# Attention scores as 64-row products of two heads in turn, with the softmax in pairs of heads

## The chip, the cores and the metric

The kernel runs on one core of a Trainium2 chip. The metric is the device time of one execution in microseconds (us); a time given for a kernel is the median of its runs. The engines have short names: PE is TensorE, DVE is VectorE, ACT is ScalarE, POOL is GpSimd, and SP (SyncE) issues the DMA transfers.

## The reference

One layer of a mixer with 128 context tokens and 512 latent tokens (8 grid rows of 64), model width 1024. A modulated RMS norm feeds one input projection; three branches read it: attention of 8 heads x 64, a gated linear recurrence, and a Fourier mixing. Each branch is gated, and one output projection, a norm and a residual follow. The change concerns the attention's scores:

```python
def one_row(r):                       # a row of the latent grid
    q_r = lax.dynamic_index_in_dim(qg, r, axis=1, keepdims=False)
    k_r = lax.dynamic_slice_in_dim(kg, r0, kh, axis=1)
    ...
    s_lat = jnp.einsum('bqhd,bjkhd->bhqjk', q_r, k_r).astype(jnp.float32) * scale
    s_lat = s_lat + bias.transpose(0, 2, 1, 3)[None].astype(jnp.float32)
    s_lat = jnp.where(col_in[:, None, :], s_lat, -jnp.inf)
    s_ctx = jnp.einsum('bqhd,bphd->bhqp', q_r, k_ctx).astype(jnp.float32) * scale
    s = jnp.concatenate([s_lat.reshape(B, H, GRID_W, kh * GRID_W), s_ctx], axis=-1)
    p = jax.nn.softmax(s, axis=-1).astype(v.dtype)
```

Everything is in float32. The 128 context tokens attend to themselves in the same way without a bias.

## The kernel before, in words

All 640 tokens are worked on together. Numbers that TensorE multiplies are kept as two parts, a main part `hi` in a rounded format and the rest `lo`; a product is then three products, hi x hi, hi x lo and lo x hi, added up in PSUM. `split` makes the two parts, a cast for the main part and a subtraction for the rest.

The program is written as streams (Python generators) that an object `Order` merges by an estimate of time: the start (modulation and norm), the recurrence, the attentions of four pairs of heads (`attention(p)`, p = 0 to 3), the gate vectors, and `fill`, which brings in the blocks of the input projection in the order of the string `FILL` and then the output projection. A block of the projection is 48 products of 320 columns (`pb<-hT,hi` and `pb<-hT,lo` in the profile, where `pb` is a PSUM bank, `hT` the modulated input, `hi`/`lo` a block of weights). Attention stands between such products. A scheduler then sets each engine's final order from a timeline of its own, and gives tiles their buffers; each engine works through its order strictly, so a product that waits holds up all of PE behind it. The numbers of buffers are in the table `WB`: `t` (21 tiles of 640 columns shared by all streams), `pe` (2 tiles for the softmax's output), `pT` (6), PSUM banks `pb` (5) and `pf` (3).

`attention_blocks(p)` prepares a pair. The two heads of a pair lie in partitions 0 to 63 and 64 to 127 (`RS[0]` and `RS[1]`). For the queries, `qd[hh]` has the main part of head hh twice, over both halves of the partitions (lines 604 and 605, two casts a head on DVE), and `qlo` the rest (line 606, POOL). For the keys, `ks[hh]` has head hh's main part in its own half and the rest in the other half (lines 618, 619), and `kcs[hh]` the same for the cached keys (631, 632). So one 128-row product of `qd[hh]` and `ks[hh]` gives hi x hi + hi x lo, and one 64-row product of `qlo` adds lo x hi. The names in the profile are `tqd`, `tqlo`, `tks`, `kc`.

`attention(p)` then goes through ten units, head 0 with four latent query tiles of 128 and the context (tile 4), then head 1. A unit is scores in one PSUM bank (256 window keys, 256 cached keys), the softmax on DVE and ACT (lines 666 to 674) into a `pe` tile, four transposes of `pe` on PE (line 118), and their split into `pT`. Two units are under way at a time, and `issue_after` holds a unit's scores behind the transposes of the unit two ahead (`AHEAD = 2`). After each head's units come its weighted values (`pb<-pT,vs`).

Of the kernel before, what the change touches and what calls it, by code (L numbers as in the profile page):

```python
# [9 lines left out]
F32 = mybir.dt.float32  # L10
F32R = mybir.dt.float32r
# [6 lines left out]
P = 128  # L18
# [8 lines left out]
WB = {"raw": 2, "hi": 3, "lo": 3, "t": 21, "pe": 2, "o": 4, "cf": 3, "pb": 5, "pf": 3, "s": 8, "m": 4, "row": 2, "tbl": 1, "pT": 6, "vs": 2, "kc": 4}  # L27
# [45 lines left out]
def mixer_kernel(ctx: ExitStack, tc: tile.TileContext, A, O):  # L73
# [37 lines left out]
    def mm(out, lhsT, rhs, start=True, stop=True):  # L111
        n, m = rhs.free_size(), lhsT.free_size()
        od.now += 1e-3 * (n * 0.4167 * 4 if rhs.dtype == F32 else max(n * 0.4167, m * 0.83)) + 2e-3
        te.matmul(out, lhsT, rhs, start=start, stop=stop)  # L114
# [5 lines left out]
    def split(src, hi, lo, hi_eng=None, lo_eng=None):  # L120
        (sc.copy if hi_eng is None else hi_eng)(hi, src)  # L121
        (ve if lo_eng is None else lo_eng).tensor_sub(lo, src, hi.bitcast(F32))  # L122

# [19 lines left out]
    # lower bounds of the forget gates: softmax and running sum over depth (one layer)  # L143
# [9 lines left out]
    def rsqrt_mean(ss, n):  # L153
        """ss -> 1/sqrt(ss/n + eps), in place."""
# [32 lines left out]
    def mod_cols(out, w):  # L187
        """[4, 128]: rows 0,1 = c_hi (w_hi + w_lo), rows 2,3 = c_lo (w_hi + w_lo)."""
# [12 lines left out]
    def mm3(out, w, k, u, first, last):  # L201
        """out += w[:, k].T @ h[k][:, half u], in three passes over the parts."""
# [92 lines left out]
    def block(name, use, lo_eng=gp):  # L295
        """128 columns of the projection; use(z, u) gets one half of the tokens, z = [128 channels, 320 tokens] in PSUM."""
# [30 lines left out]
    def twice_silu(out, z):  # L327
        """2 silu(z) = z (1 + tanh(z / 2)): tanh is in the tables of exp and of the sigmoid"""
# [10 lines left out]
    def by_token(src):  # L339
        """[128 channels, 640 tokens] -> PSUM [128 tokens, token tile, 128 channels], the first four tiles and the last."""  # L340
# [781 lines left out]
```

## Time and profile before

| | |
|---|---|
| time, median of 3 runs | 504.39 us (499.99, 504.39, 509.48) |
| profiled execution, first to last instruction | 495.5 us; its whole time is not listed by itself, and the median lies 8.9 us above this span |
| PE busy | 462.7 us, 93% |
| DVE busy | 342.9 us, 69% |
| ACT busy | 224.3 us, 45% |
| POOL busy | 195.1 us, 39% |

Durations in what follows come from the one profiled execution. A row of a timeline has the start within the span, the duration until the last of the merged instructions ends, the engine, the line, the operation, the tiles (out <- in, without buffer numbers), the shapes and the count; in brackets stands the idle time of the engine before it and what ended it. For matmuls, `64*128 64x256` means weights of 64 rows and 128 columns and a moving operand of 64 rows and 256 columns. A row of the table of stretches has the stretch, its length, the busy time and instructions of PE, of weight loads, DVE, ACT and POOL, then the granted clock of PE, and the DMA's share and rate.

### The profile page before, as it was taken

How to read it: one execution, taken by the hardware profiler on the slowest of the kernel's cores; microseconds unless marked ns; L12 is line 12 of the kernel's file. 1: busy time of each engine (PE TensorE's matmuls, PEld its weight loads, DVE VectorE, ACT ScalarE, POOL GpSimd, SP SyncE). 2: the span in 40 equal slices, each digit the busy share in tenths (PEclk: the TensorE clock that was granted, in tenths of full speed). 3: DMA queues.
4: the chain of work that ended last, by engine and by line, in shares of the span. 5: the costliest groups of instructions: out<-in, count | busy, mean ns of one | idle time of the engine just before them, and what ended most of it. 6: DMA issues, size and time to landing. Idle time of an engine off the chain costs nothing.

```text
span 495.5 us, 8372 instructions
## 1 busy us (share of the span) xinstructions
PE 462.7 (93%) x3120; PEld 417.5 (84%) x3120; DVE 342.9 (69%) x787; ACT 224.3 (45%) x561; POOL 195.1 (39%) x160
## 2 busy tenths in 40 slices
PE   3698999979999999969999999989999999999995
PEld 3677999878899999959998889879898879878884
DVE  5997857999957655683569785679673769740264
ACT  6784453625330524422524465543544555630242
POOL 2576424778451466360444213337135124130000
PEclk9858999989999999978999999999999999999998
DMA  7955414110021113110320334223243111262032
GB/s 269 392 219 196 128 47 145 44 66 0 1 63 36 50 51 104 46 50 0 91 93 13 117 102 127 83 89 112 95 150 119 44 54 44 70 232 80 2 115 97
DMA packets 19512, 47.49 MB, mean 96 GB/s; under 512 B 3196, under 2 KB 6924, under 8 KB 19472
## 3 DMA queue, kind: packets, MB, share of 16 engines
q1 hardware_dynamic: 19376, 46.94, 27.9%
q8 instruction: 24, 0.39, 0.3%
q14 instruction: 16, 0.13, 0.1%
q0 software_dynamic: 96, 0.02, 0.1%
HBM read 43.68 MB, written 3.28 MB: 95 GB/s over the span
## 4 chain that ended last, share of the span: by engine, by line
PE 66%; DVE 16%; issue 6%; DMA 5%; ACT 4%; POOL 2%; SPq 1%; POOLq 0%; DVEq 0%; ACTq 0%
PE pb L114 61%; PE pb L118 4%; DVE lo L122 3%; ACT hi L121 2%; DMA txa<-x 1%; DVE tqd L604 1%; DVE s L672 1%; DMA raw<-win 1%; DMA vs<-wss 1%; DVE tqd L605 1%; DVE t L419 1%; DMA cf<-vc 1%; DMA cf<-kc 1%; DVE pe L674 1%; DVE m L464 1%
## 5 line engine op out<-in xcount | busy, mean ns | idle before, releaser
L114 PE MATMUL pb<-hT,hi 128*128 128x320 f32 x832 | 192.1, 317 | 0.0
L114 PEld LDWEIGHTS pb<-hT,hi 128*128 128x128 f32 x832 | 140.5, 191 | 2.6 <-issue 0.2
L114 PE MATMUL pb<-hT,lo 128*128 128x320 f32 x416 | 130.9, 315 | 0.0
L122 POOL TENSOR_TENSOR lo<-raw,hi 128x1024 fp32r<-128x1024 f32 x26 | 63.8, 2456 | 93.5 <-ACT hi L121 83.0
L114 PEld LDWEIGHTS pb<-hT,lo 128*128 128x128 f32 x416 | 79.2, 190 | 0.7
L121 ACT CAST hi<-raw 128x1024 fp32r<-128x1024 f32 x46 | 48.4, 1051 | 42.9 <-PE pb L114 26.7
L114 PE MATMUL pb<-t,t 64*128 64x128 f32 (+2 forms) x414 | 55.4, 305 | 3.8 <-ACT t L452 2.9
L114 PEld LDWEIGHTS pb<-t,t 64*128 64x128 f32 (+1 forms) x414 | 46.6, 197 | 9.2 <-ACT t L452 3.1
L121 ACT CAST pT<-pb 128x256 fp32r<-128x256 f32 x64 | 23.4, 373 | 57.3 <-PE pb L118 42.5
L122 DVE TENSOR_TENSOR lo<-raw,hi 128x1024 fp32r<-128x1024 f32 x20 | 28.2, 1411 | 14.2 <-ACT hi L121 13.9
L122 DVE TENSOR_TENSOR pT<-pb,pT 128x256 fp32r<-128x256 f32 x64 | 26.3, 415 | 16.1 <-ACT pT L121 15.9
L114 PE MATMUL pb<-hi,c 128*4 128x128 f32 x192 | 29.7, 241 | 6.5 <-ACT hi L121 6.5
L114 PE MATMUL pb<-hi,mh 128*128 128x512 f32 (+1 forms) x108 | 31.9, 376 | 1.0 <-POOL mh L122 1.0
L114 PE MATMUL pb<-lo,c 128*4 128x128 f32 x192 | 29.0, 241 | 3.5 <-DVE lo L122 3.2
L118 PE MATMUL pb<-ident,pe 128*128 128x128 f32 x136 | 22.5, 285 | 4.9 <-DVE pe L674 4.9
L666 DVE TENSOR_REDUCE s<-pb 128x1 f32<-128x256 f32 x32 | 13.4, 418 | 15.3 <-PE pb L114 15.0
L114 PEld LDWEIGHTS pb<-hi,mh 128*128 128x128 f32 x108 | 19.6, 188 | 5.0 <-POOL mh L122 1.4
L114 PEld LDWEIGHTS pb<-hi,c 128*4 128x4 f32 x192 | 17.8, 93 | 6.8 <-ACT hi L121 6.5
L114 PE MATMUL pb<-pT,mh 128*128 128x512 f32 (+1 forms) x102 | 22.8, 367 | 0.0
L118 PEld LDWEIGHTS pb<-ident,pe 128*128 128x128 f32 x136 | 16.6, 145 | 6.9 <-issue 4.5
L114 PEld LDWEIGHTS pb<-lo,c 128*4 128x4 f32 x192 | 17.8, 93 | 4.9 <-DVE lo L122 3.7
L672 DVE TENSOR_TENSOR s<-s 128x1 f32<-128x1 f32 x32 | 15.1, 471 | 9.8 <-ACT pe L671 9.5
(217 smaller groups left out, 934.2 us busy)
## 6 DMA issues: line engine op xcount, KB each, us to landing
raw<-win SPq DMA_DIRECT2D x29, 512.0 KB, 3.4
raw<-wg SPq DMA_DIRECT2D x8, 512.0 KB, 3.4
raw<-wout SPq DMA_DIRECT2D x8, 512.0 KB, 3.3
vs<-wss SPq DMA_DIRECT2D x6, 512.0 KB, 5.8
raw<-wss SPq DMA_DIRECT2D x5, 512.0 KB, 5.8
pT<-wss SPq DMA_DIRECT2D x5, 512.0 KB, 5.0
t<-x SPq DMA_DIRECT2D x10, 256.0 KB, 5.3
o_y<-t SPq DMA_DIRECT2D x9, 256.0 KB, 2.0
```

Of the source, the lines that this page charges most:

```text
L114: te.matmul(out, lhsT, rhs, start=start, stop=stop)
L118: last_tr[0] = te.transpose(out, src, ident).ins
L121: (sc.copy if hi_eng is None else hi_eng)(hi, src)
L122: (ve if lo_eng is None else lo_eng).tensor_sub(lo, src, hi.bitcast(F32))
L419: ve.scalar_tensor_tensor(qb, q, 0.5, Tb, op0=ALU.mult, op1=ALU.mult)
L464: ve.tensor_mul(Tb, b1, b2)
L604: ve.tensor_copy(qd[hh][r, :], q[r, :])
L605: ve.tensor_copy(qd[hh][o, :], q[r, :])
L666: ve.reduce_max(m[:, 0:1], pss[:, 256:512], axis=AX.X)
L672: ve.tensor_add(m[:, 2:3], m[:, 2:3], m[:, 3:4])
L674: NE.tensor_scalar(pe, pe, m[:, 2:3], 0.5, op0=ALU.mult, op1=ALU.mult)
```

## The change

The queries, keys and cached keys are split like other operands: `qs`, `ks` and `kcs` are each a pair (main part, rest) with both heads in their own halves of the partitions, and `qd` and `qlo` are gone. A head's scores are three products of 64 rows, and the products of head 1 and head 0 take turns; `follow` adds an order between them. The two heads' scores go to two PSUM banks, and the softmax runs for both heads of a query tile; a unit is now a query tile of both heads, so there are five units a pair. Both heads' weighted values come after the four latent tiles' transposes, and the context's transposes after these. `WB` changes `t` from 21 to 18 and `pT` from 6 to 8. Comments are also removed, which moves line numbers: the transposes of line 118 are line 125, and `split` is in lines 127 to 129.

```diff
-WB = {"raw": 2, "hi": 3, "lo": 3, "t": 21, ..., "pT": 6, "vs": 2, "kc": 4}
+WB = {"raw": 2, "hi": 3, "lo": 3, "t": 18, ..., "pT": 8, "vs": 2, "kc": 4}
...
+    def follow(chain, ins):
+        if chain:
+            tc.add_manual_dep(ins, chain[-1].name, mybir.DependencyInfo(mybir.DependencyClass.NoSync,
+                                                                        mybir.DependencyReason.DATA), reason="turns")
+        chain.append(ins)
...
     def split(src, hi, lo, hi_eng=None, lo_eng=None):
-        (sc.copy if hi_eng is None else hi_eng)(hi, src)
+        (sc.copy if hi_eng is None else hi_eng.tensor_copy)(hi, src)
...
-            for hh in range(2):
-                r, o = RS[hh], RS[1 - hh]
-                ve.tensor_copy(qd[hh][r, :], q[r, :])
-                ve.tensor_copy(qd[hh][o, :], q[r, :])
-                QE.tensor_sub(qlo[r, :], q[r, :], qd[hh][r, :].bitcast(F32))
+            split(q, *qs, ve, QE)
...
-            for hh in range(2):
-                r, o = RS[hh], RS[1 - hh]
-                ve.tensor_copy(ks[hh][r, :], kf[r, :])
-                KE.tensor_sub(ks[hh][o, :], kf[r, :], ks[hh][r, :].bitcast(F32))
+            split(kf, *ks, ve, KE)
...
-            r, o = RS[hh], RS[1 - hh]
-            ve.tensor_copy(kcs[hh][r, :], kcf[r, :])
-            CE.tensor_sub(kcs[hh][o, :], kcf[r, :], kcs[hh][r, :].bitcast(F32))
+        split(kcf, *kcs, ve, CE)
...
-        def scores(out, hh, qt, keys):
-            cols = slice(qt * P, (qt + 1) * P)
-            mm(out, qd[hh][:, cols], keys(slice(0, P)), start=True, stop=False)
-            mm(out, qlo[RS[hh], cols], keys(RS[hh]), start=False, stop=True)
+        def scores(outs, qt, keys, chain):
+            cols, t = slice(qt * P, (qt + 1) * P), od.now
+            for n, (a, b) in enumerate(((0, 0), (0, 1), (1, 0))):
+                for hh in (1, 0):
+                    follow(chain, mm(outs[hh], qs[a][RS[hh], cols], keys(b)[RS[hh]], start=(n == 0), stop=(n == 2)))
+            od.now = 0.5 * (t + od.now)
...
-        def softmax_latent(hh, qt):
-            pss, m, pe, sb = PB(), S(4), PE_(), S(256)
-            scores(pss[:, 256:512], hh, 1 + qt, lambda r_: kcs[hh][r_, :])
...
+        def softmax_latent(qt):
+            pss, pes, chain = [PB(), PB()], [], []
+            scores([t[:, 256:512] for t in pss], 1 + qt, lambda b: kcs[b], chain)
+            scores([t[:, 0:256] for t in pss], 1 + qt, lambda b: latent_keys(b, qt), chain)
+            for hh in range(2):
+                m, pe, sb, ss = S(4), PE_(), S(256), pss[hh]
...
-        units = [(hh, qt) for hh in range(2) for qt in (0, 1, 2, 3, 4)]
...
-        for n, (hh, qt) in enumerate(units):
+        for n, qt in enumerate((0, 1, 2, 3, 4)):
             with tc.issue_after(done[n - AHEAD]) if n >= AHEAD else ExitStack():
-                pe = softmax_context(hh) if qt == 4 else softmax_latent(hh, qt)
+                pes = softmax_context() if qt == 4 else softmax_latent(qt)
...
-        yield from finish_unit(pend.pop(0))
         yield LAT["pT"]
-        weighted(1, pTs[1])
+        for hh in range(2):
+            weighted(hh, pTs[hh])
+            yield 0
+        while pend:
+            yield from finish_unit(pend.pop(0))
+            yield 0
```

The change moves instructions on several engines. First PE in pair 0. Before, the transposes of head 0's third and fourth latent tiles (`ident,pe`, four each) stand with the scores of its context (`128x128`) and those of head 1's first latent tile; the shape is that of the result:

```order
L118 MATMUL pb_2321<-ident,pe_2253 128x128 x4
L114 MATMUL pb_2330<-tks_1634,tqd_1632 128x128
L114 MATMUL pb_2330<-tks_1634,tqlo_1638 128x128
L118 MATMUL pb_2355<-ident,pe_2278 128x128 x4
L114 MATMUL pb_2364<-kc_1637,tqd_1633 128x256
L114 MATMUL pb_2364<-kc_1637,tqlo_1638 128x256
L114 MATMUL pb_2364<-tks_1635,tqd_1633 128x256
L114 MATMUL pb_2364<-tks_1635,tqlo_1638 128x256
L114 MATMUL pb_2521<-hT_108,hi_2517 128x320
```

Here each `tqd` product has 128 rows and each `tqlo` product 64. Now the fourth latent tile of both heads, still in pair 0, where every `tqs` product has 64 rows, `pb_2347` is head 1's bank and `pb_2346` head 0's:

```order
L114 MATMUL pb_2346<-kc_1636,tqs_1632 128x256
L114 MATMUL pb_2347<-kc_1637,tqs_1632 128x256
L114 MATMUL pb_2346<-kc_1637,tqs_1632 128x256
L114 MATMUL pb_2347<-kc_1636,tqs_1633 128x256
L114 MATMUL pb_2346<-kc_1636,tqs_1633 128x256
L114 MATMUL pb_2347<-tks_1634,tqs_1632 128x256
L114 MATMUL pb_2346<-tks_1634,tqs_1632 128x256
L114 MATMUL pb_2347<-tks_1635,tqs_1632 128x256
L114 MATMUL pb_2346<-tks_1635,tqs_1632 128x256
L114 MATMUL pb_2347<-tks_1634,tqs_1633 128x256
L114 MATMUL pb_2346<-tks_1634,tqs_1633 128x256
L114 MATMUL pb_2560<-hT_107,lo_2483 128x320
```

Eleven products of alternating heads stand together where units of two to four stood. The twelfth, head 1's first, stands by itself a little ahead, between projection products:

```order
L114 MATMUL pb_2560<-hT_107,lo_2483 128x320
L114 MATMUL pb_2560<-hT_107,hi_2482 128x320
L114 MATMUL pb_2347<-kc_1636,tqs_1632 128x256
L114 MATMUL pb_2560<-hT_108,hi_2482 128x320
L114 MATMUL pb_2560<-hT_107,lo_2483 128x320
```

It was moved ahead of its partner, whose PSUM bank the scheduler expected to be free later. On DVE, before, in the middle of pair 0 (the softmax of head 0's third and fourth tile, and the queries of pair 1):

```order
L667 ISA s_2277 128x1
L604 CAST tqd_2089<-tq_2088 64x640
L669 TENSOR_SCALAR s_2277<-s_2277 128x1
L605 CAST tqd_2089<-tq_2088 64x640
L122 TENSOR_TENSOR pT_2241<-pb_2267,pT_2240 128x2x128
L604 CAST tqd_2090<-tq_2088 64x640
L605 CAST tqd_2090<-tq_2088 64x640
L672 TENSOR_TENSOR s_2252<-s_2252 128x1
```

Now, at the queries of pair 1, which come after the softmax of pair 0's second tile:

```order
L678 RECIPROCAL s_2202<-s_2202 128x1
L679 TENSOR_SCALAR pe_2203<-pe_2203,s_2202 128x512
L129 TENSOR_TENSOR pT_2269<-pb_2270,pT_2268 128x2x128
L128 CAST tqs_2080<-tq_2079 128x640
L129 TENSOR_TENSOR pT_2280<-pb_2283,pT_2279 128x2x128
L671 TENSOR_REDUCE s_2306<-pb_2292 128x1
```

The four half-height casts that stood inside one softmax are one cast of full height between two softmaxes.

More of the change, by code (lines that the diff above doesn't have):

```diff
@@ L26 @@
 TOKENS = ("ir",)
-WB = {"raw": 2, "hi": 3, "lo": 3, "t": 21, "pe": 2, "o": 4, "cf": 3, "pb": 5, "pf": 3, "s": 8, "m": 4, "row": 2, "tbl": 1, "pT": 6, "vs": 2, "kc": 4}
+WB = {"raw": 2, "hi": 3, "lo": 3, "t": 18, "pe": 2, "o": 4, "cf": 3, "pb": 5, "pf": 3, "s": 8, "m": 4, "row": 2, "tbl": 1, "pT": 8, "vs": 2, "kc": 4}
 POOL_LO = (4, 7, 10, 13)
@@ L113, in mm @@
         od.now += 1e-3 * (n * 0.4167 * 4 if rhs.dtype == F32 else max(n * 0.4167, m * 0.83)) + 2e-3
-        te.matmul(out, lhsT, rhs, start=start, stop=stop)
+        return te.matmul(out, lhsT, rhs, start=start, stop=stop).ins
+    def follow(chain, ins):
[3 more added lines that the diff above has]
+        chain.append(ins)
     def tr(out, src):
@@ L569, in attention_blocks @@
         vT, q = T(), T(tag="q")
-        qd = [T(tag="qd", dt=F32R) for _ in range(2)]
+        qs = [T(tag="qs", dt=F32R) for _ in range(2)]
         ks = [T(tag="ks", dt=F32R) for _ in range(2)]
         kcs = [sp.tile([P, 256], F32R, tag="kc", name=nm("kc"), bufs=WB["kc"]) for _ in range(2)]
-        qlo = T(tag="qlo", dt=F32R)
         vs = tp.tile([P, 2, 7, P], F32R, tag="vs", name=nm("vs"), bufs=WB["vs"])
-        att[p] = (tbl, qd, ks, kcs, qlo, vs)
+        att[p] = (tbl, qs, ks, kcs, vs)
         RW = slice(0, 3), slice(3, 8)
@@ L658, in softmax_latent @@
[L658 to L675 removed]
+        tbl, qs, ks, kcs, vs = att[p]
@@ new lines, in scores, with softmax_context @@
+        def scores(outs, qt, keys, chain):
[4 more added lines that the diff above has]
+            od.now = 0.5 * (t + od.now)
+        os_ = tp.tile([P, NT], F32, tag="o", name=nm("o"), bufs=WB["o"])
+        def softmax_context():
+            pss, pes = [PB(), PB()], []
+            scores([t[:, 0:P] for t in pss], 0, lambda b: ks[b][:, 0:P], [])
+            for hh in range(2):
+                m, pe = S(4), PE_()
+                ve.reduce_max(m[:, 0:1], pss[hh][:, 0:P], axis=AX.X)
+                ve.tensor_scalar_mul(m[:, 1:2], m[:, 0:1], -1.0)
+                sc.activation(pe[:, 0:P], pss[hh][:, 0:P], ACT.Exp, bias=m[:, 1:2], accum_out=m[:, 2:3])
+                ve.reciprocal(m[:, 2:3], m[:, 2:3])
+                NE.tensor_scalar(pe[:, :P], pe[:, :P], m[:, 2:3], 0.5, op0=ALU.mult, op1=ALU.mult)
+                pes.append(pe)
+            return pes
@@ new lines, in latent_keys @@
+        def latent_keys(b, qt):
+            if qt < 3:
+                return ks[b][:, P + qt * P:P + qt * P + 256]
+            return ks[b][:, P:NT].rearrange("p (j t) -> p j t", t=P)[:, 0:4:3, :]
+        def softmax_latent(qt):
[4 more added lines that the diff above has]
+                m, pe, sb, ss = S(4), PE_(), S(256), pss[hh]
+                ve.reduce_max(m[:, 0:1], ss[:, 256:512], axis=AX.X)
+                ve.tensor_tensor_reduce(sb, ss[:, 0:256], tbl[:, int(qt == 3), hh, :], 1.0, m[:, 0:1],
+                                        op0=ALU.add, op1=ALU.max, accum_out=m[:, 1:2])
+                ve.tensor_scalar_mul(m[:, 1:2], m[:, 1:2], -1.0)
+                sc.activation(pe[:, 256:512], ss[:, 256:512], ACT.Exp, bias=m[:, 1:2], accum_out=m[:, 3:4])
+                sc.activation(pe[:, 0:256], sb, ACT.Exp, bias=m[:, 1:2], accum_out=m[:, 2:3])
+                ve.tensor_add(m[:, 2:3], m[:, 2:3], m[:, 3:4])
+                ve.reciprocal(m[:, 2:3], m[:, 2:3])
+                NE.tensor_scalar(pe, pe, m[:, 2:3], 0.5, op0=ALU.mult, op1=ALU.mult)
+                pes.append(pe)
+            return pes
```

56 lines of the change are left out of this document (15 added, 41 removed).

## The prediction

> **What bounds the kernel now.** I read the page's head first, then its chain of waits, then TensorE's timeline where the scores stand.
>
> ```profile
> span 495.5 us, 8372 instructions
> PE 462.7 (93%) x3120; PEld 417.5 (84%) x3120; DVE 342.9 (69%) x787; ACT 224.3 (45%) x561; POOL 195.1 (39%) x160
> PEclk9858999989999999978999999999999999999998
> PE 66%; DVE 16%; issue 6%; DMA 5%; ACT 4%; POOL 2%; SPq 1%; POOLq 0%; DVEq 0%; ACTq 0%
> ```
>
> TensorE (PE) is busy for 93% of the span and carries 66% of the chain. So an edit is worth what it takes from PE's instruction stream, plus or minus the waits that it takes away or makes. DVE is second, with 69%.
>
> The timeline's first column is the start. Matmuls are pipelined, so the price of one is the distance to the next start and not its duration. One group of scores stands between projection products:
>
> ```profile
> 189.74 0.31 PE L114 MATMUL pb<-hT,lo 128*128 128x320 f32 x1
> 189.89 0.28 PE L114 MATMUL pb<-kc,tqd 128*128 128x256 f32 x1
> 190.10 0.38 PE L114 MATMUL pb<-kc,tqlo 64*128 64x256 f32 x1
> 190.41 0.39 PE L114 MATMUL pb<-kc,tqd 128*128 128x256 f32 x1
> 190.72 0.38 PE L114 MATMUL pb<-kc,tqlo 64*128 64x256 f32 x1
> 191.03 0.56 PE L114 MATMUL pb<-hT,hi 128*128 128x320 f32 x2
> 191.43 0.31 PE L114 MATMUL pb<-hT,lo 128*128 128x320 f32 x1
> ...
> 119.30 0.28 PE L114 MATMUL pb<-lo,hT 128*128 128x256 f32 x1
> 119.42 0.28 PE L114 MATMUL pb<-hi,hT 128*128 128x256 f32 x1
> ```
>
> A 320-column product costs 0.147 us (189.74 to 189.89). A 256-column one costs 0.12 us among its like (119.30 to 119.42). The score products, 256 columns too, cost 0.31 us each. From 189.89 to 191.43 are 1.54 us; less two projection products (0.29) four score products took 1.25 us. At 0.12 each they would be 0.48, so 0.77 us went to the four changes between 128-row and 64-row products: **0.193 us per change of row size**.
>
> The recurrence shows what 64-row products do that lie in different halves of the rows:
>
> ```profile
> 113.99 1.16 PE L114 MATMUL pb<-t,t 64*128 64x128 f32 x8
> ...
> 140.43 1.93 PE L114 MATMUL pb<-t,t 64*128 64x128 f32 x20
> ...
> 150.74 0.83 PE L114 MATMUL pb<-t,t 128*128 128x128 f32 x6
> ```
>
> The x8 are one head's products, in one half; the x20 are both heads', partly interleaved by the scheduler. Twelve more instructions cost 0.77 us, 0.064 each. With 128 rows one costs (0.83 - 0.27) / 5 = 0.11, where 0.27 is the tail of the last. So several of the twelve ran beside one of the other half.
>
> **The change, part by part.** It is counted over PE's whole built order, at the prices above.
>
> 1. *Changes of row size.* Before, a score group alternates 128-row (`qd`) and 64-row (`qlo`) products; PE changes row size 143 times at scores. After, all scores are 64-row, and 74 changes are left. (69 x 0.193) = -13.3 us. The recurrence goes from 44 to 38 changes, because the scheduler groups its levels otherwise: -1.2 us.
> 2. *Products.* Before, 128 of 256 columns (15.4 us) and 16 of 128 columns, taken at half, 0.06 (1.0): 16.4 us. After, 192 and 24. With halves side by side, six of one head hide behind six of the other: 16 query tiles x 6 x 0.124 = 11.9 us (0.124 is 0.12 and a little for the second start), contexts 4 x 3 x 0.066 = 0.8. In 17 places the first product goes alone, ahead of its partner (the order in the section before shows one); each takes a place of its own, 17 x 0.12 = 2.0. Sum 14.7, so -1.7 us. No row has two 256-column products side by side. From both sides: full overlap makes this -1.7, no overlap makes it 192 x 0.12 + 24 x 0.06 - 16.4 = +8.1. I take the overlap, since the recurrence's rows are nearest. All this lies on PE, the bound: **-16.2 us** by 1 and 2.
>    The Trainium skill, TensorE: Matmul & The Clock Gate, section Measured speedup vs the span model, gives 3.07x for four 32-row tiles instead of 4x. An estimate from that page, the same three quarters for two halves, would stretch 12.7 us of paired products by a third, 4 us more; no run here shows 32-row tiles.
> 3. *Preparation on DVE and POOL.* Queries lose three of four half-height casts, keys one of two, cached keys one of two; POOL's two subtractions each become one of full height. It looks off the path, yet one wait of PE hangs on it:
>
> ```profile
> 205.44 2.42 POOL L122 TENSOR_TENSOR lo<-raw,hi 128x1024 fp32r<-128x1024 f32 x1 [1.33 <-ACT hi L121]
> ...
> 205.80 2.41 DVE L604 CAST tqd<-tq 64x640 fp32r<-64x640 f32 x1 [0.69 <-ACT tq L599]
> ...
> 208.29 1.57 POOL L606 TENSOR_TENSOR tqlo<-tq,tqd 64x640 fp32r<-64x640 f32 x1 [0.43 <-DVE s L669]
> 208.30 1.91 DVE L605 CAST tqd<-tq 64x640 fp32r<-64x640 f32 x1
> ...
> 210.66 0.49 DVE L604 CAST tqd<-tq 64x640 fp32r<-64x640 f32 x1
> ...
> 211.30 1.79 POOL L606 TENSOR_TENSOR tqlo<-tq,tqd 64x640 fp32r<-64x640 f32 x1 [1.44 <-DVE tqd L604]
> ...
> 211.71 1.40 DVE L672 TENSOR_TENSOR s<-s 128x1 f32<-128x1 f32 x1
> ...
> 213.17 2.34 POOL L122 TENSOR_TENSOR lo<-raw,hi 128x1024 fp32r<-128x1024 f32 x1
> ...
> 213.50 2.03 DVE L672 TENSOR_TENSOR s<-s 128x1 f32<-128x1 f32 x1
> ...
> 216.27 1.09 PE L118 MATMUL pb<-ident,pe 128*128 128x128 f32 x4 [3.87 <-DVE pe L674]
> ```
>
> ```profile
> 216.20:226.40 10.20, 10.13 (x36) 9.04 (x37) 5.44 (x20) 3.13 (x11) 3.31 (x2) 0.50 0.15 53
> 226.40:236.60 10.20, 10.20 (x63) 9.05 (x63) 4.36 (x16) 3.54 (x9) 0.90 (x1) 1.00 0.00 0
> ```
>
>    A DVE cast takes 0.49 us alone and up to 2.41 beside a POOL subtraction, and even a 128x1 addition takes 2.03. The softmax of the third query tile queued behind four such casts, and PE stood still for 3.87 us. Then the granted clock (the number behind the counts) was 0.50 for 10.2 us: 5.1 us of work lost. With one cast there, and POOL's two subtractions in one, I expect neither: **-9.0 us**. Bounds: 0 if another wait of over 3 us comes at the same place, -9.0 if not; I take the latter, as the casts were 5.3 us of that chain and one of 0.5 to 2.4 is left.
> 4. *Softmax in pairs: the added wait.* Two heads are scored at once, and transposes need both heads' `pe`, of which there are still two buffers. Behind a late transpose all of PE queues. DVE's work for one query tile, in these groups (mean ns is the number after the busy time):
>
> ```profile
> L122 DVE TENSOR_TENSOR pT<-pb,pT 128x256 fp32r<-128x256 f32 x64 | 26.3, 415 | 16.1 <-ACT pT L121 15.9
> L674 DVE TENSOR_SCALAR pe<-pe,s 128x512 f32<-128x512 f32 x32 | 19.4, 610 | 0.6
> L672 DVE TENSOR_TENSOR s<-s 128x1 f32<-128x1 f32 x32 | 15.1, 471 | 9.8 <-ACT pe L671 9.5
> L667 DVE CUSTOM_DVE_ANT_0 m<-pb,tbl,s 128x256 f32<-128x256 f32 x32 | 15.1, 475 | 0.2
> L666 DVE TENSOR_REDUCE s<-pb 128x1 f32<-128x256 f32 x32 | 13.4, 418 | 15.3 <-PE pb L114 15.0
> L673 DVE RECIPROCAL s<-s 128x1 f32<-128x1 f32 x32 | 4.9, 158 | 0.6
> L669 DVE TENSOR_SCALAR s<-s 128x1 f32<-128x1 f32 x32 | 4.5, 143 | 0.1
> ```
>
>    Two heads: 2 x (418 + 475 + 143 + 471 + 158 + 610) + 4 x 415 = 6.2 us. In pair 0's fourth query tile PE has 43 projection products (6.3 us) and four changes of row size (0.8) between the last score and the first transpose: 7.1 us. Cover is there, by a little; a POOL subtraction of 2.4 us at the wrong moment takes it. Bounds: 0, and 2.4 us at each of 16 tiles, 38 us. I take **+5 us**, 0.3 a tile, nearer to the lower end, because in this trace the same chain, with more casts in it, cost PE one wait of 3.87 and little else.
> 5. *Order and pools.* Head 0's weighting moves behind all transposes, and pair 3's last weighting now stands ahead of the last projection block, not behind it; there PE waited before:
>
> ```profile
> 430.59 0.51 PE L114 MATMUL pb<-pT,vs 128*128 128x512 f32 x1 [1.15 <-ACT pT L121]
> ```
>
>    Bounds -1.2 and 0; I take 0, since the last gate block, now later, ends in a wait of its own kind. SyncE issues the same 133 transfers, a few swapped between `raw` and `o_k`. The shared `t` buffers go from 21 to 18, `pT` from 6 to 8. PE's order up to the first score is the same but for some recurrence products, so I cost this at 0; if the recurrence lost its cover, PE would wait there for its operands.
>
> Sum: -16.2 - 9.0 + 5 = -20.2 us. The profiled span is 495.5, the median of the runs 504.39, so 8.9 us lie around the span; I leave those alone. 504.4 - 20.2 = **484 us**.
>
> **The rivals.** *No overlap.* The halves take turns without running side by side at 256 columns. Then step 2 is +8.1: -14.5 + 8.1 - 9.0 + 5 = -10.4, 494 us. The x20 row speaks against it, the other number format and width for it.
>
> *DVE sets the pace (slower).* PE's stream between score and transpose gets shorter while DVE's 6.2 us stay, so PE waits at each pair of transposes. If each of the 16 tiles waits 2.2 us (35 us), the sum is -25.2 + 35 = +10: 514 us. It decides where a tile's softmax comes later than 7.1 us after its scores; above 1.6 us a tile the gain is gone. For it: the thin cover. Against it:
>
> ```profile
> 190.00:430.00 240.00, 233.27 (x1496) 209.00 (x1494) 168.51 (x452) 114.47 (x337) 85.67 (x65) 0.98 0.25 79
> ```
>
> DVE (third pair of numbers) is busy for 168.5 of the 240 us of attention, 70%. The casts taken out are some 15 us of it, the stage loses some 25: 72%, hardly more. The Trainium skill has this rival as a rule: TensorEngine Tiling (Array Packing), section PSUM Bottleneck, says that tiling speeds up TensorE but not the emptying of PSUM, which may then bound. By that, the rows on DVE would decide, as worked out here.
>
> *The waits only move.* The 3.87 us wait and its half clock come back elsewhere (step 3 at 0), and step 4 costs 8: -16.2 + 8 = -8, 496 us.
>
> **How the numbers follow.** Forecast 0.72 (476 to 493), no overlap 0.07, waits move 0.15, DVE sets the pace 0.06. Two per cent, about what a measurement can tell from no change here, is 10 us: below 494.3 is faster. The forecast and a part of "no overlap" and "waits move" lie there: 0.79. Same 0.16, slower 0.05. The range: low, no new waits, 504.4 - 25.2 - 4 = 475, where 4 us allow for the runs' own spread (499.99 to 509.48); high, 498, which takes in both middle rivals.
>
> **What the profile after would show.** Step 1: score groups in blocks of 11 that start about 0.06 us apart, one jump of 0.2 before and one after. Step 2: about 0.85 us for such a block; 1.4 means no overlap. Step 3: a PEclk of full speed between 190 and 430, no wait of over 3 us on `pe`. Step 4: PE's waits on `pe` and `pb` below 8 us in total. Wrong, if PE's idle time in the attention stage is above 15 us, or if DVE goes above 85% there.

## The result, and the profile after

The changed kernel takes 472.09 us (median of four executions, 466.48 to 483.15) against 506.94 us for the kernel before (499.99 to 522.38) beside it: a ratio of 0.930, with a 95% interval of 0.912 to 0.949. The forecast was 484 us, with a range of 475 to 498. The direction was right, and the time fell more than was forecast: below the range.

The head of the profile after, with the rows that answer to those shown of before:

```profile
span 466.0 us, 8490 instructions
PE 440.0 (94%) x3192; PEld 404.1 (87%) x3192; DVE 313.5 (67%) x767; ACT 222.4 (48%) x561; POOL 180.6 (39%) x148
PEclk9959999997999999999999999999999999999998
PE 59%; DVE 3%; issue 1%; ACT 0%; DVEq 0%; ACTq 0%
```

PE is still the bound, busy 94% of a span that is 29.5 us shorter. The granted clock has lost its dip in the middle. The chain's row can't be set beside that of before as it stands: its shares sum to 63%, because the chain is followed back to 166 us only. Over the stretch behind 171.5 us, DVE has 12% of the chain before and 3% after, PE 76% and 94%. The profiled execution took 467.78 us, so 1.8 us lie around its span.

PE's waits behind 150 us (waiting tile and line, what it waited for, total, times, longest), first of before, then of after:

```profile
PE pb L118 <- DVE pe L674: 4.9, 3, 3.9
PE pb L114 <- DVE row L122: 1.3, 1, 1.3
PE pb L114 <- ACT pT L121: 1.1, 1, 1.1
PE pb L114 <- POOL mh L122: 1.0, 1, 1.0
PE pb L114 <- DVE t L513: 0.2, 1, 0.2
```

```profile
PE pb L114 <- DVE tg L831: 0.4, 1, 0.4
PE pb L114 <- DVE tg L337: 0.4, 1, 0.4
PE pb L114 <- DVE t L520: 0.2, 1, 0.2
```

Not only the wait of 3.9 us is gone: of 8.5 us of waits behind 150 us, 0.9 is left, and none on `pe` or `pT`. The stage that the prediction read from 190 to 430 us says the same in the table of stretches, where PE's busy time is now 239.27 of 240 us at clock 1.00, and DVE has 155 us (65%):

```profile
190.00:430.00 240.00, 239.27 (x1670) 218.54 (x1670) 154.98 (x450) 121.71 (x351) 81.77 (x63) 1.00 0.29 95
```

One unit's scores on PE's timeline, in pair 0:

```profile
200.56 0.46 PE L114 MATMUL pb<-hT,hi 128*128 128x320 f32 x2
200.85 0.31 PE L114 MATMUL pb<-hT,lo 128*128 128x320 f32 x1
201.09 0.62 PE L114 MATMUL pb<-kc,tqs 64*128 64x256 f32 x5
201.44 0.63 PE L114 MATMUL pb<-tks,tqs 64*128 64x256 f32 x6
202.00 0.56 PE L114 MATMUL pb<-hT,hi 128*128 128x320 f32 x2
```

From 200.85 to 202.00 are 1.15 us. Less the projection product (0.147) and two changes of row size (0.386), eleven products took 0.62 us, 0.056 each. That is the block of eleven with starts about 0.06 us apart that the prediction asked for; it spans 0.91 us (201.09 to 202.00), where 0.85 was said.

**Where the 29.5 us went.** Each span is divided into PE's pauses (rows like those above, over the whole span), the work lost to half clock, and PE's stream, which is what remains, counted at full clock; the first and last 6 us or so, before PE's first and behind its last matmul, stand apart.

| us | before | after | difference | forecast |
|---|---|---|---|---|
| PE's stream at full clock | 447.4 | 430.8 | -16.6 | -16.2 |
| PE's pauses | 20.3 | 12.9 | -7.4 | +1.1 |
| lost to half clock | 15.3 | 9.2 | -6.1 | -5.1 |
| before and behind PE | 12.6 | 13.1 | +0.5 | 0 |

The forecast's +1.1 is -3.9 (the wait on `pe`) and +5 (the pairs' new waits); its -5.1 is the rest of step 3. Before and after are one execution each. The stream, as what remains, is known to some 3 us: in the preparation alone and the pairs alone, which have the score products of before and nearly its changes of row size, it comes out at 443.9 and 445.0 where before has 447.4.

The medians lie 34.8 us apart and the profiled spans 29.5, because the granted clock differs between executions of one kernel: 0.908 to 0.966 in 21 executions of before that list it, 0.940 to 0.980 in after's four. So the kernels below are also compared by span times mean granted clock, a **time at full clock**, averaged over a kernel's executions. It is 478.2, 477.4 and 476.5 us for before (seven executions in each of the three series of experiments, single ones scattered by 1.4 to 1.9) and 453.9 for after (452.5 to 455.4): 23.5 us of the gain are work and waits, the other 11 or so are clock. How much of that clock belongs to the change is not shown: the ten other kernels below with after's pairs have mean clocks of 0.946 to 0.969, before of 0.932 to 0.949. Pauses don't shrink with the clock, so differences under 2 us mean nothing here.

### The profile page after: what moved, and what is told of

The parts are those of the page before. It is cut to its first block, busy times and chain, and to the rows that moved or that the text cites. A ratio compares the mean times of both kernels' runs of the same rounds, so it can differ in the third digit from the quotient of the medians.

```text
span 466.0 us, 8490 instructions
## 1 busy us (share of the span) xinstructions
PE 440.0 (94%) x3192; PEld 404.1 (87%) x3192; DVE 313.5 (67%) x767; ACT 222.4 (48%) x561; POOL 180.6 (39%) x148
## 4 chain that ended last, share of the span: by engine, by line
PE 59%; DVE 3%; issue 1%; ACT 0%; DVEq 0%; ACTq 0%
PE pb L114 55%; PE pb L125 4%; DVE t L520 1%; DVE t L810 0%; DVE vs L129 0%; DVE lo L129 0%; DVE t L949 0%; DVE pT L129 0%; ACT hi L128 0%; DVE tg L337 0%; DVE t L812 0%; DVE t L821 0%; ACT t L930 0%; DVE fin L507 0%; DVE t L817 0%
## 5 line engine op out<-in xcount | busy, mean ns | idle before, releaser
L114 PEld LDWEIGHTS pb<-hT,hi 128*128 128x128 f32 x832 | 138.8, 188 | 3.7
L114 PEld LDWEIGHTS pb<-hT,lo 128*128 128x128 f32 x416 | 78.2, 188 | 1.3
L129 DVE TENSOR_TENSOR lo<-raw,hi 128x1024 fp32r<-128x1024 f32 x20 | 25.4, 1272 | 26.6 <-ACT hi L128 26.6
L114 PE MATMUL pb<-lo,c 128*4 128x128 f32 x192 | 29.5, 240 | 4.6 <-DVE lo L129 3.2
L675 ACT ACTIVATE pe<-pb,s 128x256 f32<-128x256 f32 x32 | 15.3, 477 | 14.0 <-DVE s L674 9.8
L125 PE MATMUL pb<-ident,pe 128*128 128x128 f32 x136 | 21.0, 273 | 0.0
L686 DVE TENSOR_TENSOR o<-pb,o 64x512 f32<-64x512 f32 (+1 forms) x16 | 7.8, 487 | 19.5 <-ACT o L685 19.4
L446 DVE COPY_PREDICATED AL<-masks,pb 128x512 f32<-128x512 uint32 x28 | 20.1, 732 | 0.7 <-PE pb L114 0.7
```

Of the source, the lines that this page charges most:

```text
L114: return te.matmul(out, lhsT, rhs, start=start, stop=stop).ins
L125: last_tr[0] = te.transpose(out, src, ident).ins
L446: ve.copy_predicated(out, mk.to_broadcast([P, i1 - i0, P]), pa[:, :w].rearrange("p (a t) -> p a t", t=P))
L675: sc.activation(pe[:, 256:512], ss[:, 256:512], ACT.Exp, bias=m[:, 1:2], accum_out=m[:, 3:4])
L686: ve.tensor_add(out, src[r, :], out)
```

## The experiments

All in one table: the pauses are PE's behind 150 us, and the stream is that of the profiled execution.

| kernel | median us | time at full clock | pauses | stream |
|---|---|---|---|---|
| before | 506.94 | 477.4 | 8.5 | 447.4 |
| after | 472.09 | 453.9 | 0.9 | 430.8 |
| preparation alone | 491.91 | 472.9 | 4.1 | 443.9 |
| pairs alone | 501.45 | 472.2 | 4.0 | 445.0 |
| before, rest queries padded to 128 rows | 486.40 | 457.9 | 13.3 | 422.1 |
| after, heads not in turn | 482.08 | 459.7 | 3.6 | 434.3 |
| after, old casts and subtractions | 491.09 | 464.2 | 10.6 | 429.6 |
| after, old casts | 475.62 | 459.5 | 4.9 | 430.7 |
| after, old subtractions | 477.74 | 454.8 | 1.9 | 431.2 |
| after, `pb` 6 and `pf` 2 | 493.18 | 468.4 | 18.0 | 426.1 |
| after, scores in one tile of two banks | 482.34 | 461.8 | 7.4 | 430.4 |
| grouped by row size | 481.22 | 458.9 | 12.1 | 425.6 |
| grouped, one query copy on ACT | 473.87 | 453.4 | 6.1 | 424.1 |
| grouped, query, key and cached-key copies on ACT | 473.49 | 452.3 | 5.5 | 424.3 |

### The preparation alone

The kernel before, its units and order kept, with one cast and one subtraction an operand:

```diff
-                ve.tensor_copy(qd[hh][r, :], q[r, :])
-                ve.tensor_copy(qd[hh][o, :], q[r, :])
-                QE.tensor_sub(qlo[r, :], q[r, :], qd[hh][r, :].bitcast(F32))
+            ve.tensor_copy(qd[0], q)
+            QE.tensor_sub(qlo, q, qd[0].bitcast(F32))
```

(and keys and cached keys likewise). It leaves out the copies that keep the two heads apart, so its scores are not the attention's; the number and shape of the products are those of before.

> The kernel before, with the change's preparation alone: one full-height cast and one subtraction for queries, keys and cached keys. Scores, units and product shapes stay as before, but both heads use the same main part of the queries, and the keys' rest has both heads' rows, so the scores are not the attention's. PE changes row size 144 times at scores, as before. Theory 1 (the casts made the wait of 3.87 us and the half clock behind it): about 9 us less than before, and PE's idle time in the attention stage falls by 4 us or more. Rival (the preparation is off the path, the gain is all in the products): within 2 us of before, the wait stays or moves.

Measured: median 491.91, ratio 0.970 (0.958 to 0.981); at full clock 472.9, 5.3 us below before. Its waits behind 150 us hold none on `pe`:

```profile
PE pb L114 <- DVE tg L330: 2.2, 1, 2.2
PE pb L114 <- DVE t L122: 1.0, 1, 1.0
PE pb L114 <- ACT pT L121: 0.7, 1, 0.7
PE pb L114 <- DVE t L513: 0.2, 1, 0.2
```

So the casts' part of the mechanism holds: without them the 3.9 us on `pe` are gone. But waits of 2.2 and 1.0 us on other tiles take a part back in this order of the work, so the preparation is worth some 5 us alone (its four executions lie between 470.1 and 476.1), where about 9 were expected.

### The pairs alone

The units of after, with the products and the preparation of before:

```diff
-            split(q, *qs, ve, QE)
+            for hh in range(2):
+                ve.tensor_copy(qd[hh][r, :], q[r, :])
+                ve.tensor_copy(qd[hh][o, :], q[r, :])
+                QE.tensor_sub(qlo[r, :], q[r, :], qd[hh][r, :].bitcast(F32))
...
+            for hh in (1, 0):
+                follow(chain, mm(outs[hh], qd[hh][:, cols], keys(hh), start=True, stop=False))
+                follow(chain, mm(outs[hh], qlo[RS[hh], cols], keys(hh)[RS[hh]], start=False, stop=True))
```

> The changed kernel's units (both heads of a query tile, softmax in pairs, weighting after all transposes, its buffers), with the products and the preparation of before: 128 rows, then 64, head after head, four casts for the queries. 144 changes of row size at scores, as before. Theory 1 (the units only add waits): 0 to 5 us slower than before, and the wait at the casts may stay. Rival (the units took PE's waits away): 8 us or more faster than before, with PE's idle time in the attention stage below 2 us.

Measured: median 501.45, ratio 0.998 (0.990 to 1.006), a granted clock of 0.941 to 0.953; at full clock 472.2, 6.0 below before. Neither expectation came true, the 0 to 5 us more nor the 8 us less. The waits behind 150 us:

```profile
PE pb L125 <- DVE pe L689: 2.3, 3, 1.4
PE pb L125 <- ACT pT L128: 0.6, 1, 0.6
PE pb L114 <- DVE pT L129: 0.3, 1, 0.3
```

This is the sharpest test of step 4, since here the pairs' softmax has all the old casts beside it and no shorter products. PE's wait on `pe` went from 4.9 to 2.3 us, and all pauses behind 150 us from 8.5 to 4.0. Scoring two heads at once adds no wait by itself. The old casts made no wait as long as that of 3.87 us here either, so they make one only where the order lets them.

### The old preparation in the kernel after

There are three variants: the old number of casts and subtractions (each query half cast twice, as before), the old casts with single subtractions, and single casts with the old subtractions.

```diff
-            split(q, *qs, ve, QE)
+            for hh in range(2):
+                r = RS[hh]
+                for _ in range(2):
+                    ve.tensor_copy(qs[0][r, :], q[r, :])
+                QE.tensor_sub(qs[1][r, :], q[r, :], qs[0][r, :].bitcast(F32))
```

```diff
-            split(q, *qs, ve, QE)
+            for hh in range(2):
+                r = RS[hh]
+                for _ in range(2):
+                    ve.tensor_copy(qs[0][r, :], q[r, :])
+            QE.tensor_sub(qs[1], q, qs[0].bitcast(F32))
```

```diff
-            split(q, *qs, ve, QE)
+            ve.tensor_copy(qs[0], q)
+            for r in RS:
+                QE.tensor_sub(qs[1][r, :], q[r, :], qs[0][r, :].bitcast(F32))
```

Keys and cached keys are treated likewise, with each half cast once.

> The changed kernel with the preparation's old price: four half-height casts for the queries (two of them written twice with the same values), two for the keys and two for the cached keys, and two subtractions each; same values, same products, 72 changes of row size against 74. Theory 2 (each of three things, preparation, pairs and shorter scores, gives PE's waits room, and any one suffices for most of it): PE's idle time behind 150 us stays below 4 us, and the time at equal clock is within 4 us of the changed kernel. Rival (the casts alone made the waits): the idle time comes back to 7 us or more, 7 us slower.

> The changed kernel with the old number of DVE casts (four half-height for the queries, two for the keys, two for the cached keys) and the new number of POOL subtractions (one each); the same values and products. Theory 4 (DVE's own casts fill the softmax's cover): most of the 10 us by which the kernel with both old parts stood above the changed kernel, 6 us or more. Rival (it is POOL's second subtraction that slows DVE beside it): 3 us or less.

> The changed kernel with one full-height DVE cast for each operand, as in the change, and the old number of POOL subtractions (two of half height each); the same values and products. Theory 4 (DVE's casts make the waits): within 3 us of the changed kernel at equal clock. Rival (POOL's second subtraction makes them): 6 us or more above it.

Measured at full clock: both +10.3 us against after, the casts alone +5.6, the subtractions alone +0.9. So the first met its rival, the second fell a little short of the 6 us of its theory, and the third met its theory. The streams stay within 1.2 us of after's, while the pauses behind 150 us grow by 9.7, 4.0 and 1.0 us. Waits behind 150 us of the kernel with both, then of that with the casts:

```profile
PE pb L125 <- DVE pe L689: 8.3, 5, 5.0
PE pb L125 <- DVE s L688: 1.4, 2, 1.1
```

```profile
PE pb L125 <- DVE pe L689: 2.0, 1, 2.0
PE pb L114 <- ACT pe L685: 1.0, 1, 1.0
```

The longest of the first, on DVE's, POOL's and PE's timeline:

```profile
221.75 0.47 DVE L623 CAST tks<-tk 64x640 fp32r<-64x640 f32 x1
222.15 0.15 DVE L688 RECIPROCAL s<-s 128x1 f32<-128x1 f32 x1
222.30 1.57 POOL L624 TENSOR_TENSOR tks<-tk,tks 64x640 fp32r<-64x640 f32 x1 [6.30 <-DVE s L688]
222.32 4.21 DVE L623 CAST tks<-tk 64x640 fp32r<-64x640 f32 x1
223.84 2.35 POOL L129 TENSOR_TENSOR lo<-raw,hi 128x1024 fp32r<-128x1024 f32 x1
226.57 1.83 DVE L637 CAST kc<-cf 64x256 fp32r<-64x256 f32 x2
...
228.43 0.89 DVE L689 TENSOR_SCALAR pe<-pe,s 128x512 f32<-128x512 f32 x1
...
229.47 1.09 PE L125 MATMUL pb<-ident,pe 128*128 128x128 f32 x4 [4.96 <-DVE pe L689]
```

The first key cast takes 0.47 us. The second starts with POOL's subtraction of the first half, takes 4.21 us beside two POOL subtractions (the second is of the projection's weights), and ends 0.3 us behind the second of them; it and the cached keys' casts stand ahead of the softmax's last step, and PE stands still for 4.96 us. This is the wait of before come back at another operand. It is what step 4 feared, and its full size needs the old casts and subtractions together: a second cast that a subtraction of the first half runs beside. The pairs alone had both and waited for `pe` only 2.3 us, with a longer stream on PE; whether the shorter stream or another place in the order makes that difference was not separated. The edits interact: in the kernel before the new preparation was worth 5 us, here 10.

### The heads not in turn

```diff
-            for n, (a, b) in enumerate(((0, 0), (0, 1), (1, 0))):
-                for hh in (1, 0):
+            for hh in (1, 0):
+                for n, (a, b) in enumerate(((0, 0), (0, 1), (1, 0))):
```

> The changed kernel, with the order of the score products alone altered: three products of head 1, then three of head 0, where they took turns. 68 changes of row size at scores against 74. Theory 1 (halves run side by side when heads take turns): a group of six takes 5 places of 0.12 us where 3 were taken, 32 groups x 0.24 = 7.7 us and 0.5 for the contexts, less 1.2 us for six changes of row size: about 7 us slower than the changed kernel. Rival (only the changes of row size count, the halves never overlap at 256 columns): 1 us faster to no difference, and the spacing of score products is 0.12 us in both.

Measured: 459.7 at full clock, 5.8 above after: stream +3.5, pauses behind 150 us +2.7. That is near the 7 us of the first theory, but by luck, for its reason is not what happened. Had the halves stopped running side by side, the stream would have grown by about 10 us (step 2's two ends, -1.7 and +8.1). They did not stop. Written is: three `kc` products of head 0, three `tks` of head 1, three `tks` of head 0, in nine successive instructions. The timeline has them so:

```profile
199.82 0.31 PE L114 MATMUL pb<-hT,hi 128*128 128x320 f32 x1
200.06 0.38 PE L114 MATMUL pb<-kc,tqs 64*128 64x256 f32 x1
200.07 0.38 PE L114 MATMUL pb<-tks,tqs 64*128 64x256 f32 x1
200.28 0.28 PE L114 MATMUL pb<-kc,tqs 64*128 64x256 f32 x1
200.29 0.28 PE L114 MATMUL pb<-tks,tqs 64*128 64x256 f32 x1
200.40 0.28 PE L114 MATMUL pb<-kc,tqs 64*128 64x256 f32 x1
200.41 0.62 PE L114 MATMUL pb<-tks,tqs 64*128 64x256 f32 x4
200.96 0.42 PE L114 MATMUL pb<-hT,hi 128*128 128x320 f32 x1
```

The starts are paired 0.01 us apart: head 1's first product starts with head 0's first, though two others of head 0 stand ahead of it. Each half works through its own products, and only the last three, which have no partner, run alone, 0.12 us apart. So the overlap is shown, and in this case it hangs on both halves having work close by in the program, not on strict turns.

### No change of row size at all

The kernel before, with the rest of each query padded with zeros to 128 rows, so that no score product has 64 (static query tiles, `t` 17):

```diff
-            mm(out, qlo[RS[hh], cols], keys(RS[hh]), start=False, stop=True)
+            mm(out, qlo[hh][:, cols], keys(slice(0, P)), start=False, stop=True)
```

> The kernel before, where the second product of each score has 128 rows too: the rest of the queries lies in tiles whose other half is zero. So PE never changes row size at scores (0 against 144), and nothing overlaps. Single-head units, four casts for the queries, and 17 shared tiles where there were 21 (the padded tiles take their room). Theory 1 (a change of row size costs 0.193 us wherever it stands): 144 x 0.193 = 27.8 us off PE's stream, so 25 to 30 us faster than before, and score products 0.12 us apart. Rival (pairs and halves side by side are what pays): at most 10 us faster than before, PE waiting for the softmax instead.

Measured: median 486.40, ratio 0.959 (0.944 to 0.975); at full clock 457.9, 20.3 below before. The same four products between two projection products, which took 1.25 us:

```profile
188.75 0.31 PE L114 MATMUL pb<-hT,lo 128*128 128x320 f32 x1
188.90 0.28 PE L114 MATMUL pb<-kc,tqd 128*128 128x256 f32 x1
189.02 0.28 PE L114 MATMUL pb<-kc,qp 128*128 128x256 f32 x1
189.13 0.28 PE L114 MATMUL pb<-kc,tqd 128*128 128x256 f32 x1
189.25 0.28 PE L114 MATMUL pb<-kc,qp 128*128 128x256 f32 x1
189.37 0.46 PE L114 MATMUL pb<-hT,hi 128*128 128x320 f32 x2
```

Now 0.47 us (188.90 to 189.37), 0.12 each, with no less arithmetic. Changes of row size in the whole program go from 187 to 36, and the stream shrinks by 25.3 us, 0.168 a change; the prediction's 0.193 from one place is a little high as a mean, and why stays open. The old casts stay, and pauses of 13.3 us, 5.8 of them on `pe`, eat a part, so the 25 to 30 us that were expected did not come out. PE's stream got 25 us shorter and DVE's work did not: this looks like the rival "DVE sets the pace", in a mild form.

### Banks

After with `WB` at `pb` 6, `pf` 2; and after with both heads' scores in one tile of two banks (`pb` 3 and one such tile).

```diff
-WB = {..., "pb": 5, "pf": 3, ...}
+WB = {..., "pb": 6, "pf": 2, ...}
```

```diff
-WB = {..., "pb": 5, "pf": 3, ...}
+WB = {..., "pb": 3, "pf": 3, "pd": 1, ...}
...
-            pss, pes, chain = [PB(), PB()], [], []
+            pss, pes, chain = PD(), [], []
```

> The changed kernel with six PSUM banks for the shared tag and two for the projections, where it had five and three. The first score product goes alone in 8 places instead of 17, and 60 changes of row size are left at scores instead of 74 (88 instead of 112 over all). Theory 1: 24 x 0.193 = 4.6 us and nine places of 0.12 less, so 5 to 6 us below the changed kernel at equal clock, if two banks are enough for the projections. Rival (projections then wait for their banks): PE idles 3 us or more behind 45 us, and the time is the same or longer.

> The changed kernel with the two heads' scores in one PSUM tile of two banks (a buffer of its own, three single banks are left beside it), so both heads' banks come free together and no first product goes alone: 48 changes of row size at scores against 74, though 58 in the recurrence against 38, 106 over all against 112. Theory 3 (a product that goes alone costs a place and two changes, but the free banks it uses are worth more): the stream is 2 us shorter, and PE's waits in the attention stage and the recurrence grow by 3 us or more, so slower than the changed kernel at equal clock. Rival (the lone products are a pure loss): 2 to 6 us below the changed kernel.

Measured at full clock: +14.5 and +7.9 us against after, with pauses of 18.0 and 7.4. Neither split is free. In the first, the stream is 4.7 us shorter, as its fewer changes of row size let expect, but projection blocks wait for their fewer banks: four waits on the gates' `tg`, 5.8 us in all, the longest 3.1, and one on `pe` of 2.8. The second was slower, as expected, by its pauses; its stream is no shorter. So of these three ways to share the banks, the five and three of the changed kernel is the best.

### Grouped by row size

Pairs with the old operands, but four 128-row products and then four 64-row products in turns: 40 changes of row size at scores, after has 74. First with the old preparation, then with the second query copy on ACT, then with key and cached-key copies there too.

```diff
+            for hh in (1, 0):
+                for n, keys in enumerate(keyss):
+                    follow(chain, mm(outs[hh][n], qd[hh][:, cols], keys(hh), start=(n == 0), stop=False))
+            for n in range(len(keyss)):
+                for hh in (1, 0):
+                    follow(chain, mm(outs[hh][n], qlo[RS[hh], cols], keyss[n](hh)[RS[hh]], start=False, stop=(n == len(keyss) - 1)))
...
-                ve.tensor_copy(qd[hh][o, :], q[r, :])
+                sc.copy(qd[hh][o, :], q[r, :])
```

> The changed kernel's units with the products of before in another order: for a query tile first the four 128-row products of both heads, then the four 64-row products, heads in turn; the preparation is that of before (four casts for the queries). 40 changes of row size at scores against 74 in the changed kernel, 128 + 16 products instead of 192 + 24. Theory 1 (PE's stream and its waits add up): 34 fewer changes are -6.6 us, the products come to about the same, PE's waits are 3 us longer because of the casts: 3 to 6 us below the changed kernel at equal clock. Rival (the second half of the gain was the cheaper preparation): 0 to 5 us above the changed kernel.

> As the grouped kernel (128-row products of both heads, then 64-row products in turn), with the copy of the queries' main part into the other half done on ACT instead of DVE: two half-height casts for the queries on DVE instead of four. 40 changes of row size at scores. Theory 1 (DVE's casts beside POOL make PE's waits): PE idles 2 us or more less than the grouped kernel in the attention stage, and the time at equal clock is 6 to 8 us below the changed kernel. Rival (a wait on ACT takes its place): the same as the grouped kernel or slower.

> The grouped kernel (four 128-row products of both heads, then four 64-row products in turn, 40 changes of row size at scores) with the queries' second copy and the keys' and cached keys' main parts cast on ACT: DVE casts are left for the queries' own half alone. Theory 4 (DVE's casts make PE's waits): PE's idle time behind 150 us falls from 6.1 to 3 us or less, and the time at equal clock is 3 us below the changed kernel, 450 or 451. Rival (ACT's casts delay the exponentials instead): 453 or more.

Measured at full clock: 458.9, 453.4 and 452.3. The stream is 5 to 7 us shorter than after's, and pauses of 12.1, 6.1 and 5.5 us give it back. None of the gains of 3 to 8 us below after that were expected came. The query copy on ACT took 5.5 us off the first of them, and more waits stayed than was expected. The last is level with after (453.9, median 473.49 against 472.09): a shorter stream with more waits. No kernel here beats the changed one by more than these numbers can tell.

## Why the prediction was right or wrong

**Steps 1 and 2** held: -16.6 us measured against -16.2, though an agreement to 0.4 us is luck with a stream that is known to some 3 us. The block of eleven, the heads not in turn and the padded kernel show both parts, the price of a row-size change and the overlap at 256 columns; how the 16.6 us divide between them was not separated. The Trainium skill's 3.07x for four tiles (TensorE: Matmul & The Clock Gate, section Measured speedup vs the span model), read as three quarters for two halves, would by the prediction's estimate have made the stream 4 us longer; the trace disagrees, since eleven products at 0.056 us are a little under half of 0.12 each. The rival "no overlap" is out.

**Step 3** had the right mechanism and about the right size in this kernel: the 3.87 us wait is gone, and with it the half clock of 5.1 us behind it. (The other 1.0 of the -6.1 lies in the half clock at 21 to 35 us, ahead of the first score.) The preparation alone removes all waits on `pe`, and putting the old one back brings one of 4.96 us. But the casts are not enough for such a wait: the pairs alone have them all, and their longest wait on `pe` is 1.4 us.

**Step 4** is the step that failed: +5 us for new waits of the pairs, measured 0. The prediction set DVE's 6.2 us a tile against 7.1 us of PE's work, called the cover thin, and chose 0.3 us a tile. The pairs alone show that this comparison does not give the waits: there the same sum is 6.1 us a tile, hardly less, and PE's pauses behind 150 us fell from 8.5 to 4.0. Two parts of it were off. The 7.1 us left out the eight transposes of the tile before and the six score products of the context, which PE does in the same stretch: at that tile, 8.3 us lie between the end of the last score and the first transpose (210.1 to 218.4). Over the 16 latent query tiles after it is 6.6 to 12.6 us, 8.5 in the median, and in the pairs alone 6.9 to 17.5, 11.2 in the median. And of the 6.2 us, 1.7 are the splits into `pT`, which come behind the tile's own transposes.

It could seem that DVE's rows before were only stretched by the casts and subtractions that step 3 removes. The same groups after, and behind them the scaling with the preparation alone:

```profile
L679 DVE TENSOR_SCALAR pe<-pe,s 128x512 f32<-128x512 f32 x32 | 16.0, 501 | 0.8
L672 DVE CUSTOM_DVE_ANT_0 m<-pb,tbl,s 128x256 f32<-128x256 f32 x32 | 14.5, 474 | 0.0
L671 DVE TENSOR_REDUCE s<-pb 128x1 f32<-128x256 f32 x32 | 12.3, 416 | 11.2 <-PE pb L114 11.2
L677 DVE TENSOR_TENSOR s<-s 128x1 f32<-128x1 f32 x32 | 7.2, 226 | 12.5 <-ACT pe L676 11.7
```

```profile
L668 DVE TENSOR_SCALAR pe<-pe,s 128x512 f32<-128x512 f32 x32 | 22.7, 709 | 0.7
```

After, the additions fell from 471 to 226 ns and the scaling from 610 to 501. Two heads now need 2 x (416 + 474 + 143 + 226 + 161 + 501) + 4 x 414 = 5.5 us (143, 161 and 414 are the means of the shift, the reciprocal and the split in the same table). But with the preparation alone the scaling is longer than before, the addition is 350 ns, and the sum stays at 6.2 us. In the kernel after with the old casts and subtractions it is 5.9, and PE's pauses are 10.6 us where after has 0.9. So the length of the softmax's own steps does not decide. What the timelines of the two long waits show instead, 3.87 us before and 4.96 us here, is casts that stand ahead of these steps on DVE. Of the 32 scalings, those that end less than 0.5 us ahead of their transposes on PE are six before, six in the pairs alone and seven in each of the two kernels that put the old casts back into after; they are four with the old subtractions alone, one in after and none in the preparation alone. The sum treated steps 3 and 4 as independent, and they are not. Nor did the pairs need the new preparation to come out even, as the pairs alone show.

**Steps 3 and 5** left out the other waits. Behind 150 us before also had 1.0 us on `pe` in two smaller waits, 1.3 on `row`, 1.1 on `pT`, 1.0 on `mh`: 4.4 us. The prediction named one of them (1.15 at 430.59), bounded it by -1.2 and 0, and took 0; it came out at the other end. All four went, and 0.8 us on `tg` came. What moved each was not tried singly; in the preparation alone three went and 3.2 us came elsewhere, so which small waits survive depends on the order as a whole.

**The base** was the other error: 8.9 us were said to "lie around the span". It is 1.8 us (467.78 and 466.0 here, 497.75 and 496.0 in an execution of before). The rest was lower granted clock in the timed executions, which is not a constant: after's mean is 0.963, before's 0.949, 0.933 and 0.932 in the three series. The forecast for the median kept what lies between before's profiled execution and its median (7.1 us) for after too, where it is 4.3: 2.8 of the 12.1 us by which the forecast missed. From 495.5 + 1.8 - 20.2 the forecast for a profiled execution would have been 477.1; it took 467.78. Of these 9.3 us, 8.5 are the pauses, 1.0 the half clock, 0.4 the stream, and 0.5 go the other way.

**The rivals.** "DVE sets the pace" is excluded for after: DVE is busy 65% from 190 to 430 us, where it was 70%, and PE waits for almost nothing there. The rival shows in the kernels that shorten PE's stream and keep the old casts, with pauses of 10.6 to 13.3 us. The rule of the Trainium skill behind it (TensorEngine Tiling (Array Packing), section PSUM Bottleneck: tiling does not speed up the emptying of PSUM) did not decide here. "The waits only move" is what the changed kernel with the old casts and subtractions does, and after does not.

## What to carry to other kernels

Where a wait is feared, count everything that the waiting engine has to do meanwhile, and at all places (7.1 us were counted at one tile where the trace has 8.3), and ask what stands ahead of the late step in its engine's queue before summing the step's own parts. When two edits touch the same queue, price the second with the first already made: the preparation was worth 5 us in the kernel before and 10 in the kernel after. On the engine at the bound, count changes of row size like instructions, and keep work for both halves of the rows close by in the program. Look for the cause of a short wait in DVE operations that run beside POOL, and compare kernels at one granted clock before explaining the last ten microseconds.

## What the runs showed of the hardware that was not expected

**Half clock lasts differently after the same wait.** In after and in the preparation alone, PE waits 2.9 us for the same tile of the recurrence at about 105 us. In the preparation alone half clock sets in only 5.4 us behind that wait, and 0.6 behind another of 1.2 us. The stretch behind it, after and then the preparation alone (the number behind the counts is the granted clock):

```profile
106.50:113.50 7.00, 6.27 (x36) 5.83 (x36) 7.00 (x15) 4.14 (x12) 5.59 (x6) 0.51 0.01 2
```

```profile
110.00:160.00 50.00, 48.79 (x229) 43.09 (x228) 27.82 (x70) 14.11 (x36) 16.73 (x18) 0.53 0.00 1
```

Half clock lasted 6.8 us in one and 51.2 in the other, with PE busy for 48.8 of the 50 us shown; 3.4 us with the heads not in turn, 27.3 with the old casts, all behind waits of 2.9 us there. The second row costs some 25 us of work and is most of why its profiled execution is long. The Trainium skill (TensorE: Matmul & The Clock Gate, section What's actually happening) gives at least one busy window of about 3.4 us until full clock is back. The lengths here agree with that step: they are 1, 2, 8 and 15 times 3.41 us. What sets their number was not found.

**Half clock without a long wait.** In the pairs alone, whose scores of two heads are eight products that change between 128 and 64 rows, half clock set in twice in the attention, at 318.3 and 366.1 us, for 6.8 us each. In the 3.4 us ahead PE had waited 0.55 us the first time and not at all the second, but it had changed row size 8 and 11 times. At the prediction's 0.193 us a change, an estimate, 1.5 and 2.1 us went to the changes. The 1.64 us wait at 44 us of before, with half clock behind it at 45.5, is of that size. Whether changes of row size bring on half clock as waits do is not shown, but if so, they cost more than their own time.

**Row halves queue by themselves.** The rows above of the heads not in turn show starts that are not in program order. The Trainium skill (TensorE: Matmul & The Clock Gate, section The mechanism) says that matmuls start strictly in order; in this trace the starts of products in different row halves don't. So "each engine works through its order strictly", as the kernel before was described, is too strong for PE: products of one half started here ahead of earlier ones of the other half.

**DVE beside POOL.** A cast of 64x640 took 0.47 us alone and 4.21 us beside two POOL subtractions. The Trainium skill (GPSIMD Engine Reference, section 1. Specifications) says that the two engines share their way into the on-chip memory, with contention for some forms of DVE instructions; the rows agree, with a ninefold time here, though no run shows whether the cast is of such a form.
